# A two-block float32 network on one core: instruction order taken from the framework's time-line simulation, modulation tiles moved out of the SSD mixer

## The chip, the cores and the metric

The kernel runs on one core of one Trainium2 chip. The core has a matrix engine (TensorE, PE in the profile), a vector engine (VectorE, DVE), an activation engine (ScalarE, ACT), a general engine (GpSimd, POOL) and DMA queues, here issued by SyncE (SP). Each engine works through one list of instructions in the order in which the list was written; engines wait for each other by semaphores. The metric is the device time of one execution in microseconds. Before the change it is 1647.56 us, the median of three runs (1647.04 to 1647.98).

## The reference, cut to what matters

512 tokens of 1024 float32 channels pass two blocks.

```python
# block 1
mod = silu(c) @ w_ada + b_ada                 # 6 x 1024 numbers: shift, scale and gate, twice
h = rms_norm(x, norm1_w) * (1 + scale1) + shift1
q, k, v, xBC, z, dt_raw, gates = split(h @ w_in)
attn = block_attention(rope(norm(q)), rope(norm(k)), v)      # 16 heads, 4 k/v heads
ssd  = ssd_mixer(xBC, z, dt_raw, ...)         # conv + SiLU, 4 groups of 8 heads, both directions,
                                              # chunks of 128, times SiLU(z), rms_norm
merged = sigmoid(ga) * (attn @ w_attn_out) + sigmoid(gs) * (ssd @ w_ssd_out)
x = x + gate1 * (merged @ w_o)
x = x + gate2 * (square(relu((rms_norm(x) * (1 + scale2) + shift2) @ w_mlp1)) @ w_mlp2)
# block 2
x = x + rglru_layer(x)     # conv, gated linear recurrence
x = x + mla_layer(x)       # attention with compressed k/v, 8 heads
return rms_norm(x, final_norm)
```

## The kernel before, in words

All large products are float32 made of three products in a shorter format: `mm3` (L172) issues L174 (high by high), L175 and L176 (the two cross terms). A weight tile of 512 KB comes by DMA into the buffer pool `wr`, ACT casts its high part (L162, `wh`), and DVE or POOL subtracts the low part (L165, `wl`). The three pools have four buffers each. Every product of 512 columns accumulates in a PSUM tile `pm`, of which there are four; other results in PSUM are named `px`, `pf`, `pg`.

The modulation numbers `mod` are 48 columns of `modc`. Each is made by `mod_tiles` (L274): one DMA of a 512 KB tile of `w_ada` into a buffer of the pool `wr`, and one DVE instruction with an accumulated sum (L279). Columns 0 to 15 are needed for `h`, at the start. Columns 16 to 47 are needed only behind the merge, where `mod_cols` (L1380) and `gate_rows` (L934) read them. `MODS` (L43) says how many of them are made in each of the four SSD groups: 0, 0, 6 and 10. Attention makes the next eight and the merge one in each of its eight steps.

The SSD mixer runs over four groups. `ssd_core` (L553) goes through the steps of `CORE` (L41), and between them `ssd` (L676) issues the *fill*: products that nothing in this group waits for soon (`xbc` and `z` of the next group, `ssd_out` of the one before). The steps are states S, mixers M and outputs Y:

```python
# S: state of one chunk
nc.tensor.matmul(p, lhsT=Btm[:, c], rhs=xw, ...)                         # L598, xw by DVE L596
self.e("st").tensor_tensor(out=v8(st), in0=v8(prev[d]), in1=dcy, ...)    # L603 (DVE)
nc.vector.tensor_tensor(out=st, in0=st, in1=p, op=ALU.add)               # L604
nc.tensor.matmul(p, lhsT=CT[:, ...], rhs=st, ...)                        # L608
# M: mixer of one head: PE pf, pg (L623); per chunk ACT L629, DVE L631, ACT, DVE L635;
#    then ACT exp L642 and POOL e = e * w (L643)
# Y: output of two heads: PE L650, L653 (reads both e); then
nc.vector.scalar_tensor_tensor(out=yd, in0=xsT[j], ..., in1=y, ...)      # L657
nc.vector.scalar_tensor_tensor(out=yd, in0=yd, ..., in1=zt, ...)         # L659
nc.scalar.activation(out=hi, in_=yd, func=AF.Identity, scale=nw)         # L669, yh
nc.vector.scalar_tensor_tensor(out=lo, in0=yd, ..., in1=r32(hi), ...)    # L670, yl
```

`ssd_out` multiplies all four pairs (yh, yl) of a group by weights. In attention a head is four score products (L844, L845 into `px`), row maxima on DVE (L755), exponentials on ACT, scaling on POOL (L763), sixteen transposes (L851), the split into `ph` (ACT) and `pl` (DVE, L170), and the products with v (L859, L860). Its fill is q/k/v of the next k/v head and the gate products.

The order of instructions on each engine is not that of the source. When the `TileContext` of L1523 closes, the framework's scheduler orders them all, with the source's order as priority, and writes one list per engine.

Of the kernel before, what the change touches and what calls it, by code (L numbers as in the profile page):

```python
# [39 lines left out]
AORD = "s0 s1 s2 s3 f0 t0 m0 t1 m1 t2 m2 t3 m3 f1".split()  # L40
CORE = "S0 S1 M0 S2 S3 M1 S4 S5 M2 M3 Y0 M4 M5 Y1 M6 M7 Y2 Y3"  # L41
NC = 19
MODS = [0, 0, 6, 10]  # L43
WP = 0
TP = 0
LO = {"start": 5, "ssd": 8, "attn": 2, "merge": 3, "mlp": 0, "rglru": 3, "mla_in": 6, "mla": 5}
# [13 lines left out]
class Build:  # L60
# [616 lines left out]
    def ssd(self, first):  # L677
# [22 lines left out]
        for g in range(4):  # L700
# [5 lines left out]
            else:  # L706
# [3 lines left out]
                fill = so + zs + [lambda: next(q0, None)] * Q0  # L710
            k0 = 16 + sum(MODS[:g])
            k1 = k0 + MODS[g]
            fill = [lambda f=f, i=i: (f(), self.mod_tiles([k0 + i] if k0 + i < k1 else [])) for i, f in enumerate(fill)]
# [123 lines left out]
    def attention(self):  # L837
        nc = self.nc

        def scores(h, t):  # L840
            stk, (kh, kl), vv = self.qk[h // 4]
            p = self.ps()
            s = slice(t * 128, t * 128 + 128)
            nc.tensor.matmul(p, lhsT=stk[h % 4][:, s], rhs=kh, start=True, stop=False)  # L844
            nc.tensor.matmul(p, lhsT=stk[h % 4][:, s], rhs=kl, start=False, stop=True)  # L845
            return self.softmax_tile(p, 512)

        def turn(pr, kt):
            p = self.ps()
            for t in range(NT):  # L850
                nc.tensor.transpose(out=p[:, t * 128:t * 128 + 128], in_=pr[t][:, kt * 128:kt * 128 + 128],  # L851
                                    identity=self.ident)
            ph, pl = self.t("ph", F32R), self.t("pl", F32R)
            self.split(ph, pl, p)
            return ph, pl

        def mix(h, po, kt, parts):
            vv, (ph, pl) = self.qk[h // 4][2], parts
            nc.tensor.matmul(po, lhsT=vv[:, kt], rhs=ph, start=kt == 0, stop=False)  # L859
            nc.tensor.matmul(po, lhsT=vv[:, kt], rhs=pl, start=False, stop=kt == 3)  # L860

        def output(h, po):

            if h % 2 == 0:
                self.of = self.t("of")
            of = self.of
            d = slice(64 * (h % 2), 64 * (h % 2) + 64)
            e = slice(64 * (1 - h % 2), 64 * (1 - h % 2) + 64)
            nc.scalar.copy(out=of[d], in_=po[e])
            nc.vector.tensor_tensor(out=of[d], in0=of[d], in1=po[d], op=ALU.add)  # L870
            if h % 2 == 1:
                self.split(self.oh[:, h // 2], self.ol[:, h // 2], of)

        gates = [lambda m=m: self.gate_ssd(m) for m in range(8)]
        mods = list(range(16 + sum(MODS), 40))

        def fill(what):
            with self.fills():
                for x in what:
                    if x == "q":  # L880
                        next(nxt, None)
                    elif x == "g" and gates:
                        gates.pop(0)()
                    elif x == "m" and mods:
                        self.mod_tiles([mods.pop(0)])

        pr = [scores(0, t) for t in range(NT)]
        for h in range(16):
            g, i = divmod(h, 4)
            if i == 0:  # L890
                nxt = self.qkv(g + 1) if g < 3 else iter(())
            last = pr
            if i == 3:
                fill("q" * 8)
            pr = []
            po = self.pm() if POM else self.ps()
            turned = {}
            for x in AORD:
                j = int(x[1])
                if x[0] == "s" and h < 15:  # L900
                    pr.append(scores(h + 1, j))
                elif x[0] == "t":
                    turned[j] = turn(last, j)
                elif x[0] == "m":
                    mix(h, po, j, turned.pop(j))
                elif x[0] == "f":
                    fill(ATT[g][2 * i + j])
            output(h, po)
        fill("g" * 8 + "m" * len(mods))

    def merge(self):
        nc, a = self.nc, self.a
        oh, ol, acc, mh, ml = self.oh, self.ol, self.accS, self.mh, self.ml
        for m in range(8):
            gt = []
            self.gate_tile(m, gt)
            th = gt[0]

            def evac(i, ps):
                nc.vector.scalar_tensor_tensor(out=th, in0=th, scalar=1.0, in1=ps, op0=ALU.add, op1=ALU.mult)  # L920
                nc.vector.tensor_tensor(out=th, in0=th, in1=acc[:, m], op=ALU.add)
                self.split(mh[:, m], ml[:, m], th)

            self.gemm_cm([[a["w_attn_out"][m]]], lambda k: (oh[:, k], ol[:, k]), evac)
            self.mod_tiles([40 + m])

    def gate_rows(self, j, s):
        nc, a = self.nc, self.a
# [598 lines left out]
```

## Time and profile before

| | |
|---|---|
| median of three runs | 1647.56 us |
| the profiled execution | 1645.17 us |
| its span, first to last instruction | 1643.4 us |
| mean granted clock of TensorE | 0.995 |
| busy: PE / DVE / ACT / POOL | 96% / 69% / 48% / 27% |

The span is one execution seen by the profiler; 1.8 us lie around it. PE is busy nearly throughout, so the time is PE's work and the short pauses in it. The stages by time: modulation, norm and first products up to about 80 us, the SSD mixer to about 500, attention to about 720, the merge to about 840, then output projection, MLP and block 2.

### The profile page before, as it was taken

The page shows a single profiled execution, that of the slowest core. Times are in us where ns is not written, and L with a number is a line of the kernel's source. Part 1 is how long each engine was busy: PE and PEld are TensorE (multiplying, and loading weights), DVE is VectorE, ACT ScalarE, POOL GpSimd, SP SyncE. Part 2 cuts the span into 40 slices and gives each one's busy share as a digit, 9 for nine tenths or more (in the row PEclk, how much of TensorE's full clock was granted, in tenths as well). Part 3 has the DMA queues.
Part 4 walks back from the last instruction along what each step waited for, and adds up shares of the span by engine and source line. Part 5 has one row for each costly group of instructions (what it writes and reads, how often), then busy time and mean ns, then how long its engine had stood idle before and what let it go on. Part 6 is the DMA issues. An engine that isn't in the chain of part 4 may idle for free.

```text
span 1643.4 us, 20885 instructions
## 1 busy us (share of the span) xinstructions
PE 1579.3 (96%) x7696; PEld 1279.9 (78%) x7696; DVE 1126.8 (69%) x1948; ACT 789.5 (48%) x1517; POOL 446.5 (27%) x322
## 2 busy tenths in 40 slices
PE   5989999999999999999999999999999999999998
PEld 3767677677688778778889888888888778988886
DVE  6899689689869988874454344343458884747873
ACT  4347546355465667663344232322337662455652
POOL 3414345254252344321133011111141011321012
PEclk9999999999999999999999999999999999999999
DMA  7511124224222222215323232323323222322211
GB/s 255 197 57 60 52 87 130 66 82 146 78 77 91 71 71 90 78 52 192 103 64 116 90 103 91 102 90 103 112 70 99 87 90 67 100 69 71 64 62 52
DMA packets 50648, 153.54 MB, mean 93 GB/s; under 512 B 8177, under 2 KB 12913, under 8 KB 50546
## 3 DMA queue, kind: packets, MB, share of 16 engines
q1 hardware_dynamic: 50546, 152.22, 28.9%
q8 instruction: 60, 0.98, 0.2%
q14 instruction: 42, 0.34, 0.1%
HBM read 150.10 MB, written 2.10 MB: 93 GB/s over the span
## 4 chain that ended last, share of the span: by engine, by line
PE 72%; DVE 16%; ACT 4%; issue 3%; POOL 3%; DMA 1%; SPq 0%; DVEq 0%; POOLq 0%; ACTq 0%
PE pm L174 19%; PE pm L175 19%; PE pm L176 19%; DVE acc L507 2%; PE px L608 1%; DVE wada L279 1%; DVE nmax L755 1%; DVE wl L165 1%; PE px L851 1%; PE px L598 1%; POOL rs L254 1%; DVE w L635 1%; PE px L860 1%; PE px L653 1%; PE px L650 1%
## 5 line engine op out<-in xcount | busy, mean ns | idle before, releaser
L162 ACT CAST wh<-wr 128x1024 fp32r<-128x1024 f32 (+5 forms) x245 | 239.5, 980 | 390.3 <-PE pm L175 176.0
L165 DVE TENSOR_TENSOR wl<-wr,wh 128x1024 fp32r<-128x1024 f32 (+2 forms) x170 | 201.6, 1187 | 182.3 <-ACT wh L162 181.6
L165 POOL TENSOR_TENSOR wl<-wr,wh 128x1024 fp32r<-128x1024 f32 (+3 forms) x75 | 175.9, 2347 | 530.6 <-ACT wh L162 483.3
L174 PE MATMUL pm<-hh,wh 128*128 128x512 f32 (+1 forms) x432 | 172.9, 404 | 7.9 <-ACT hh L169 6.2
L175 PE MATMUL pm<-hl,wh 128*128 128x512 f32 (+1 forms) x432 | 175.0, 405 | 3.4 <-POOL hl L170 3.4
L176 PE MATMUL pm<-hh,wl 128*128 128x512 f32 (+1 forms) x432 | 172.4, 399 | 0.0
L986 POOL TENSOR_TENSOR r<-r 128x512 f32<-128x512 f32 x32 | 50.9, 1589 | 252.3 <-ACT r L985 252.3
L174 PE MATMUL pm<-h,wh 128*128 128x512 f32 (+1 forms) x288 | 105.4, 366 | 0.0
L175 PE MATMUL pm<-h,wh 128*128 128x512 f32 (+1 forms) x288 | 105.2, 365 | 0.0
L176 PE MATMUL pm<-h,wl 128*128 128x512 f32 (+1 forms) x288 | 105.2, 365 | 0.0
L174 PEld LDWEIGHTS pm<-hh,wh 128*128 128x128 f32 (+1 forms) x432 | 81.2, 188 | 29.4 <-ACT hh L169 7.6
L175 PEld LDWEIGHTS pm<-hl,wh 128*128 128x128 f32 (+1 forms) x432 | 81.6, 189 | 26.1 <-POOL hl L170 6.3
L174 PE MATMUL pm<-wh,rh 128*128 128x512 f32 x256 | 99.8, 390 | 0.0
L763 POOL TENSOR_SCALAR pr<-pr,psum 128x512 f32<-128x512 f32 x64 | 64.6, 1021 | 129.1 <-DVE psum L759 71.1
L176 PE MATMUL pm<-wh,rl 128*128 128x512 f32 x256 | 99.6, 389 | 0.0
L175 PE MATMUL pm<-wl,rh 128*128 128x512 f32 x256 | 99.6, 389 | 0.0
L176 PEld LDWEIGHTS pm<-hh,wl 128*128 128x128 f32 (+1 forms) x432 | 81.5, 189 | 19.7 <-issue 3.1
L507 DVE SCALAR_TENSOR_TENSOR acc<-pm,conv_w_s,acc 128x510 f32<-128x510 f32 (+2 forms) x114 | 84.5, 741 | 9.0 <-ACT acc L498 8.0
L643 POOL TENSOR_TENSOR e<-e,w 128x512 f32<-128x512 f32 x32 | 52.0, 1625 | 100.5 <-ACT e L642 74.5
L279 DVE SCALAR_TENSOR_TENSOR wada<-wada,cs 128x1024 f32<-128x1024 f32 x48 | 66.3, 1390 | 15.6 <-DMA wada<-in_w_ada 15.3
L758 ACT ACTIVATE pr<-px,nmax 128x512 f32<-128x512 f32 (+2 forms) x96 | 60.4, 637 | 29.9 <-DVE nmax L755 24.0
L174 PE MATMUL pm<-ha,wh 128*128 128x512 f32 (+1 forms) x192 | 68.2, 355 | 0.0
(401 smaller groups left out, 4130.1 us busy)
## 6 DMA issues: line engine op xcount, KB each, us to landing
wr<-in_w_mlp SPq DMA_DIRECT2D x64, 512.0 KB, 3.4
wada<-in_w_ada SPq DMA_DIRECT2D x48, 512.0 KB, 3.9
wr<-in_w_xbc SPq DMA_DIRECT2D x24, 512.0 KB, 3.5
wr<-in_w_in_a SPq DMA_DIRECT2D x20, 512.0 KB, 3.5
wr<-in_w_z SPq DMA_DIRECT2D x16, 512.0 KB, 3.5
wr<-in_w_ssd_out SPq DMA_DIRECT2D x16, 512.0 KB, 3.5
wr<-in_w_gate SPq DMA_DIRECT2D x16, 512.0 KB, 4.0
wr<-in_w_qkv SPq DMA_DIRECT2D x16, 384.0 KB, 3.1
```

Of the source, the lines that this page charges most:

```text
L162: nc.scalar.copy(out=hi[:, :n], in_=raw[:, :n])
L165: eng.tensor_tensor(out=lo[:, :n], in0=raw[:, :n], in1=r32(hi[:, :n]), op=ALU.subtract)
L174: m(out, lhsT=lh, rhs=rh, start=start, stop=False)
L175: m(out, lhsT=lh, rhs=rl, start=False, stop=False)
L176: m(out, lhsT=ll, rhs=rh, start=False, stop=stop)
L254: g.tensor_tensor(out=r, in0=r, in1=self.mhalf.to_broadcast(list(ss.shape)) if len(ss.shape) == 2 else self.mhalf.unsqueeze(2).to_broadcas ...
L279: nc.vector.scalar_tensor_tensor(out=w, in0=w, scalar=1.0, in1=self.cs, op0=ALU.mult, op1=ALU.mult, accum_out=self.modc[:, j:j + 1])
L507: nc.vector.scalar_tensor_tensor(out=acc[:, lo:hi], in0=ps[:, lo + o:hi + o], scalar=w[:, j:j + 1], in1=acc[:, lo:hi], op0=ALU.mult, op1=A ...
L643: self.e("ew").tensor_tensor(out=e, in0=e, in1=w, op=ALU.mult)
L758: nc.scalar.activation(out=e[:, :n], in_=p, func=AF.Exp, bias=nmax, accum_out=s)
L763: self.e("norm").tensor_scalar(out=e[:, :n], in0=e[:, :n], scalar1=s, scalar2=1.0, op0=ALU.mult, op1=ALU.mult)
L986: self.e("sq").tensor_tensor(out=r, in0=r, in1=r, op=ALU.mult)
```

## The change

`MODS` becomes all zeros, so that no modulation tile is made in the SSD groups; attention makes columns 16 to 23; each merge step makes three columns in place of one, 24 in all in place of eight. `TileContext` is given `schedule_with_timeline_sim=True`: the framework's scheduler then orders the instructions by its time-line simulation. What is computed is the same: the same count of instructions on each engine (PE 7420, DVE 1902, ACT 1375, POOL 327, SP 354), in another order.

```diff
-MODS = [0, 0, 6, 10]
+MODS = [0, 0, 0, 0]
...
-        mods = list(range(16 + sum(MODS), 40))
+        mods = list(range(16, 24))
...
             self.gemm_cm([[a["w_attn_out"][m]]], lambda k: (oh[:, k], ol[:, k]), evac)
-            self.mod_tiles([40 + m])
+            self.mod_tiles([24 + m, 32 + m, 40 + m])
...
-    with tile.TileContext(nc) as tc:
+    with tile.TileContext(nc, schedule_with_timeline_sim=True) as tc:
         emit(tc, a, out)
```

Three places show the order on PE. The numbers behind names tell buffers apart; where a number is the same before and after, it is the same tile, and `hh_102`, `hl_103` are the two parts of `h`.

The first place is the state steps of SSD group 0. Before, PE's list there (`pm_1138` is a fill product):

```order
L598 MATMUL px_907<-xw_905,Btm_720 128x512
L176 MATMUL pm_1059<-hh_102,wl_1062 128x512
L174 MATMUL pm_1138<-hh_102,wh_1140 128x512
L175 MATMUL pm_1138<-hl_103,wh_1140 128x512
L176 MATMUL pm_1138<-hh_102,wl_1141 128x512
L174 MATMUL pm_1138<-hh_102,wh_1140 128x512
L175 MATMUL pm_1138<-hl_103,wh_1140 128x512
L176 MATMUL pm_1138<-hh_102,wl_1141 128x512
L608 MATMUL px_912<-st_909,th_635 128x512
L623 MATMUL pf_951<-csb,sel 128x512
```

After, the states of the steps S3, S4 and S5 and the mixers beside them:

```order
L598 MATMUL px_907<-xw_905,Btm_720 128x512
L608 MATMUL px_912<-st_909,th_635 128x512
L623 MATMUL pf_951<-csb,sel 128x512
L623 MATMUL pg_952<-csb,sel 128x512
L598 MATMUL px_977<-xw_975,Btm_720 128x512
L608 MATMUL px_982<-st_979,th_635 128x512
L598 MATMUL px_1027<-xw_1025,Btm_720 128x512
L608 MATMUL px_1032<-st_1029,th_635 128x512
L623 MATMUL pf_1035<-csb,sel 128x512
L623 MATMUL pg_1036<-csb,sel 128x512
L623 MATMUL pf_1093<-csb,sel 128x512
L623 MATMUL pg_1094<-csb,sel 128x512
```

In the new list L598 and the L608 that needs its result stand side by side, and the fill that stood around them stands earlier; in groups 1 to 3 the new list has some 5 to 7 us of PE's work between the two.

The second place is behind output Y0 of the same group (`px_1117`). Before:

```order
L653 MATMUL px_1117<-e_955,xtm_695 64x128
L650 MATMUL px_1117<-ident,yoff_776 128x128
L653 MATMUL px_1117<-e_833,xtm_695 64x128
L653 MATMUL px_1117<-e_955,xtm_695 64x128
L623 MATMUL pf_1178<-csb,sel 128x512
L174 MATMUL pm_1307<-hh_102,wh_1309 128x512
L175 MATMUL pm_1307<-hl_103,wh_1309 128x512
L623 MATMUL pg_1179<-csb,sel 128x512
L176 MATMUL pm_1307<-hh_102,wl_1310 128x512
L174 MATMUL pm_1307<-hh_102,wh_1309 128x512
```

After:

```order
L653 MATMUL px_1117<-e_833,xtm_695 64x128
L653 MATMUL px_1117<-e_955,xtm_695 64x128
L650 MATMUL px_1117<-ident,yoff_776 128x128
L653 MATMUL px_1117<-e_833,xtm_695 64x128
L653 MATMUL px_1117<-e_955,xtm_695 64x128
L623 MATMUL pf_1178<-csb,sel 128x512
L623 MATMUL pg_1179<-csb,sel 128x512
L623 MATMUL pf_1202<-csb,sel 128x512
L623 MATMUL pg_1203<-csb,sel 128x512
L174 MATMUL pm_1495<-yh_1134,wh_1490 128x512
L174 MATMUL pm_1509<-yh_1134,wh_1490 128x512
L174 MATMUL pm_1548<-yh_1134,wh_1543 128x512
```

Before, 68 rows of fill, mixers and the next output follow the last L653 of Y0 until `yh_1134` is read. After, it is read by the fifth row: the four L623 alone stand between. `pm_1495`, `pm_1509`, `pm_1548` and `pm_1562` are four products of `ssd_out`, one row of each in turn.

The third place is a head in attention. Before, behind its score products (`px_5804` is the last):

```order
L175 MATMUL pm_5818<-wl_5827,hh_102 128x384
L176 MATMUL pm_5818<-wh_5826,hl_103 128x384
L844 MATMUL px_5804<-stk_5401,stk_5530 128x512
L845 MATMUL px_5804<-stk_5409,stk_5530 128x512
L174 MATMUL pm_5817<-wh_5832,hh_102 128x384
L175 MATMUL pm_5817<-wl_5833,hh_102 128x384
L176 MATMUL pm_5817<-wh_5832,hl_103 128x384
L174 MATMUL pm_5817<-wh_5832,hh_102 128x384
L175 MATMUL pm_5817<-wl_5833,hh_102 128x384
```

After, another head (`px_5999` is its last score):

```order
L844 MATMUL px_5989<-stk_5353,stk_5545 128x512
L845 MATMUL px_5989<-stk_5361,stk_5545 128x512
L844 MATMUL px_5999<-stk_5353,stk_5545 128x512
L845 MATMUL px_5999<-stk_5361,stk_5545 128x512
L851 MATMUL px_6044<-ident,pr_5731 128x128
L851 MATMUL px_6044<-ident,pr_5741 128x128
L851 MATMUL px_6044<-ident,pr_5751 128x128
L851 MATMUL px_6044<-ident,pr_5761 128x128
L859 MATMUL px_5968<-ph_6049,v_5286 128x512
```

Before, rows of a q/k/v product (`pm_5817`, `pm_5818`) stand between the scores of a head and its transposes. After, the transposes of this head follow its scores at once, and no `pm` row stands in the whole head; six heads in all stand so, in three pairs, and the fill is gathered ahead of each pair.

## Rows read from the trace of the kernel before

**Rows 1.** The page's first two lines: span, busy time and instructions of each engine.

```profile
span 1643.4 us, 20885 instructions
PE 1579.3 (96%) x7696; PEld 1279.9 (78%) x7696; DVE 1126.8 (69%) x1948; ACT 789.5 (48%) x1517; POOL 446.5 (27%) x322
```

**Rows 2.** The page's chain that ended last, shares by engine.

```profile
PE 72%; DVE 16%; ACT 4%; issue 3%; POOL 3%; DMA 1%; SPq 0%; DVEq 0%; POOLq 0%; ACTq 0%
```

**Rows 3.** PE's waits: tile, line, releaser; us in all, times, longest.

```profile
PE px L608 <- DVE st L604: 6.9, 5, 2.5
PE px L844 <- DVE of L870: 3.8, 3, 1.4
PE px L471 <- issue: 3.3, 1, 3.3
PE px L807 <- DVE st L170: 2.8, 4, 1.4
PE px L598 <- DVE xw L596: 2.6, 2, 1.4
PE px L860 <- DVE pl L170: 2.0, 4, 0.9
PE pm L175 <- DVE yl L670: 1.8, 1, 1.8
PE pm L174 <- DVE acc L507: 1.7, 1, 1.7
PE px L653 <- POOL e L643: 1.3, 1, 1.3
```

**Rows 4.** Windows: length, busy time (instructions) per engine, granted clock, DMA share, GB/s.

```profile
80.00:500.00 420.00, 401.26 (x1882) 301.08 (x1880) 352.18 (x625) 219.54 (x481) 164.07 (x82) 0.99 0.26 82
720.00:840.00 120.00, 119.97 (x560) 98.04 (x559) 58.98 (x81) 44.04 (x69) 18.20 (x14) 1.00 0.36 119
960.00:1000.00 40.00, 40.00 (x178) 33.13 (x177) 13.90 (x15) 15.68 (x22) 12.51 (x8) 1.00 0.31 95
```

**Rows 5.** The same view, three windows of 4 us behind two pauses of PE.

```profile
92.00:96.00 4.00, 1.61 (x7) 1.55 (x7) 2.95 (x4) 0.38 (x2) 1.02 (x1) 0.79 0.44 131
96.00:100.00 4.00, 4.00 (x22) 3.41 (x21) 3.66 (x9) 3.21 (x7) 0.00 (x0) 0.78 0.00 0
172.00:176.00 4.00, 4.00 (x18) 2.79 (x18) 1.91 (x3) 1.91 (x4) 0.00 (x0) 0.61 0.01 3
```

**Rows 6.** Timeline, first SSD output: start, duration, engine, line.

```profile
143.52 0.44 PE L653 MATMUL px<-e,xtm 128*64 128x128 f32 x4
...
144.50 0.74 DVE L657 SCALAR_TENSOR_TENSOR yd<-th,ssd_D_s,px 128x512 f32<-128x512 f32 x1
...
145.28 2.33 POOL L643 TENSOR_TENSOR e<-e,w 128x512 f32<-128x512 f32 x1 [1.89 <-DVE yd L657]
145.76 0.68 DVE L659 SCALAR_TENSOR_TENSOR yd<-yd,zt 128x512 f32<-128x512 f32 x1
...
146.96 1.73 DVE L165 TENSOR_TENSOR wl<-wr,wh 128x1024 fp32r<-128x1024 f32 x1
147.01 0.71 ACT L669 ACTIVATE yh<-yd,ssd_norm_w_s 128x512 fp32r<-128x512 f32 x1
148.61 0.74 DVE L670 SCALAR_TENSOR_TENSOR yl<-yd,ssd_norm_w_s,yh 128x512 fp32r<-128x512 f32 x1
```

**Rows 7.** DVE by line and form: count, busy us, mean ns, idle before.

```profile
L279 DVE SCALAR_TENSOR_TENSOR wada<-wada,cs 128x1024 f32<-128x1024 f32 x48 | 66.3, 1390 | 15.6 <-DMA wada<-in_w_ada 15.3 <-issue 0.2
L170 DVE TENSOR_TENSOR pl<-px,ph 128x512 fp32r<-128x512 f32 x72 | 48.2, 685 | 9.7 <-ACT ph L169 8.6
L755 DVE TENSOR_REDUCE nmax<-px 128x1 f32<-128x512 f32 x72 | 47.5, 680 | 9.4 <-PE px L845 8.9
L604 DVE TENSOR_TENSOR st<-st,px 128x512 f32<-128x512 f32 x16 | 10.9, 681 | 0.9 <-PE px L598 0.6
```

**Rows 8.** The page's groups: the POOL product that ends a mixer.

```profile
L643 POOL TENSOR_TENSOR e<-e,w 128x512 f32<-128x512 f32 x32 | 52.0, 1625 | 100.5 <-ACT e L642 74.5
```

## The prediction

> **What bounds the kernel now.** I read the page's first lines, then the chain, then PE's waits, then windows. PE is busy 1579.3 of 1643.4 us [rows 1], and PE has 72% of the chain, DVE 16% [rows 2]; so 64 us of pauses is all that an order can win, and every pause that it adds counts in full. Where PE has no pause, 178 matmuls fill 40.00 us [rows 4], 0.225 us for one of 512 columns; that is my price for a row of fill. The waits show where the pauses are [rows 3]: in the SSD mixer the state steps (L608 behind L604, 6.9 us; L598, 2.6), 3.3 us ahead of L471, and 4.8 at its outputs and mixers (L175 behind yl 1.8, L174 behind acc 1.7, L653 behind e 1.3); in attention 8.6 (L844 3.8, L807 2.8, L860 2.0). DVE is the second engine: in the SSD stretch it is busy 352 of 420 us, 84% [rows 4].
>
> The sum is made against the profiled execution, 1645.17 us; the median of the runs is 2.4 us above it, and I add that at the end.
>
> **State steps.** In the new list groups 1 to 3 have 5 to 7 us of PE's work between an L598 and its L608. L604 takes 0.68 us [rows 7] and no wait there was longer than 2.5 [rows 3], so those waits go: 6.9 + 2.6 = 9.5. In group 0, three pairs stand side by side with no work between. The least price of a pair is L604's 0.68, the most 2.5; I take 1.2 and 3.6 for the three, since DVE has other work there. Net -5.9, between -7.5 and -2.0.
>
> **L471.** The new list has 24 rows of fill ahead of it, 5.4 us of work, against a pause of 3.3; that goes. [...] Net -5.0; none of it if the fill ahead of it merely moves the pause.
>
> **Outputs.** This is the largest term. The fill that covered them stands earlier, ahead of the states and mixers. One output's chain as it ran [rows 6]: the last L653 ends at 143.96, yh is ready at 147.72, yl at 149.35, 5.4 us later. The first four rows that read yh (four `pm` tiles, 0.9 us) need no yl, so PE needs 4.5 us of other work between the last L653 and the first reader. Counted over the new list at 0.225 a row, it has, for the four outputs of each group: 0.9, 0.9, 2.9, 4.0 (group 0), 9.8, 1.6, 4.3, 4.0, then 12.8, 3.0, 4.3, 4.0, and 0.9, 0.9, 2.3, 3.0 (group 3). What lacks to 4.5 adds up to 9.3 + 3.6 + 2.2 + 10.9 = 26.0. The same count over the list before has 4.0, 4.0 and 4.1 as its least and gives 1.4, where 1.8 was measured [rows 3]: so the 4.5 is about right. What was late inside the chain was DVE's queue: an L165 of 1.73 us stood ahead of L670 [rows 6]. Lower bound: with nothing queued the chain is its four instructions, 0.74 + 0.68 + 0.71 + 0.74, and 0.54 of start, 3.4; PE then needs 2.5, and 7.7 us are lacking. Upper bound: another 1.1 us of DVE's queue, 5.6, and some 41 are lacking. I take 26.0, nearest to the measured chain. A second count agrees: from mixer 1 to the last yl of group 0, DVE has 36 us of work at its mean durations, PE 24; from mixer 2 in group 3, 36 against 22. DVE works in order, so PE cannot be done sooner. The 4.8 us of waits there before are part of this count and are taken off: net +21.2, between +2.9 and +36.
>
> [...] In the new list the outputs stand close to the mixers, so L659 and L670 (two inputs in SBUF) meet POOL's L643. One such meeting is shown: L643 began at 145.28 and took 2.33 us [rows 6] against a mean of 1.63 [rows 8], and L659, begun second, took 0.68 within it. So POOL was slowed by 0.7 us and DVE not held. [...]
>
> **Attention.** Six heads in three pairs stand without fill. In the third pair, from the first score of the one head to the last pl of the next product, DVE's new list has 8 L755 (0.68), 11 L170 (up to 0.685), 3 L279 (1.39) [rows 7] and 16 short ones: about 17 to 19 us, less 0.07 each where neighbours overlap; PE has 12 there. Excess 5 to 7 us; the other pairs give 4.1 and 4.5. I take 14, in place of the 8.6 of waits before: +5.4. Between -4 (DVE runs ahead during the bursts of fill) and +13 (the last heads, also nearly bare, wait as well).
>
> **The modulation tiles.** 16 tiles leave the SSD groups and join the merge: 16 x 1.39 = 22 us of DVE and 8.4 MB. From 720 to 840 us DVE is busy 59 of 120, the DMA engines 0.36 at 119 GB/s [rows 4], or 14.3 MB in 43 us of transfer; 8.4 MB more make 69 of 120. Both have room, and merge PE work hides them. But the tiles pass through the four buffers of `wr` that also bring the weights: +2, between 0 and +8. The freed DVE time in groups 2 and 3 is in the counts above; where it lets every queue drain, it is in the lower bounds.
>
> **Clock.** A pause of PE is followed by a fall: the two windows above, and 0.61 in the window behind L653's wait, 0.39 x 4 = 1.6 us [rows 5]. That second pause is one of those counted off. With the new pauses of 3 to 4 us I expect three more falls: 3 x 1.7 - 1.6 = +3.4, between -1.6 and +7.
>
> **Sum.** -5.9 - 5.0 + 21.2 + 5.4 + 2 + 3.4 = +21.1. 1645.2 + 21.1 + 2.4 = 1668.7, so 1669 us, 1.3% slower. All lower bounds: -15; all upper: +62 (L471 at 0). The stages behind the merge barely move; I price them at 0.
>
> **Rivals.**
> 1. *The waits go and the outputs are absorbed* (faster). DVE has 22 us less in groups 2 and 3, so its queue may be empty when an output comes. If the chain from L653 to yl is 3.4 us rather than 5.4 and the bare heads cost no more than the 8.6 before, the sum is the lower bounds: 1645 - 15 + 2.4, about 1632. It decides from some 10 us of lacking cover downwards. For it: the state waits surely go. Against: DVE's own count in groups 0 and 3.
> 2. *POOL and DVE hold each other* (much slower): if each of L659 and L670 waits for a whole L643 of 1.63, the six outputs with under 2 us of cover wait 6 x 2 x 1.63 = 20 us more: 1688. [...] Against it is the L659 that ran in 0.68 us [rows 6].
> 3. *The buffers of wr bind the merge*: if the three modulation tiles of a step hold the weights back by one L279 each (1.39 a step, 8 steps), 11 more: 1680. For it: four buffers, and a tile is freed only by DVE in its order. Against: DVE is half idle there.
> 4. *The pauses only move*: what the states and L471 give, 11 us, is what outputs and heads take, with the output term between its lower bound and mine: 1645 to 1650, no change (within 0.2%, about what a measurement of this kernel can tell).
>
> **How the numbers follow.** Forecast 0.50, rival 1 0.22, rival 2 0.10, rival 3 0.09, rival 4 0.09. The forecast's own range, outputs lacking 12 to 32 and the rest by up to 10 more, is 1655 to 1685. For 8 in 10 the range takes in rival 4, most of rivals 2 and 3, and the upper half of rival 1: 1637 to 1692. Faster by over 0.2% (below 1644.3): 0.22; within: 0.09; slower (above 1650.9): 0.69.
>
> **What would show it.** In the new profile: L608 behind L604 under 4 us and only in group 0; no pause at L471; L174 and L175 behind yh and yl as the largest group of PE's waits, 20 us or more, in groups 0 and 3; L844, L860 and L851 behind DVE and ACT in three places of attention; granted clock below 1 in more windows of the SSD stretch. I am wrong if PE's busy share stays at 96%, if the yh and yl waits stay under 8 us, or if the time is lost in the merge or behind it.

## The result, and the profile after

The changed kernel takes 1769.12 us (median of four runs; 1767.49 to 1771.28), against 1647.31 before (the three runs given above and one more): 1.074 times as long (95% interval 1.0721 to 1.0758). The prediction had the direction and about a sixth of the size: 1669 us, between 1637 and 1692.

The first lines of the page after answer to [rows 1]; span, then busy time and instructions of each engine:

```profile
span 1766.5 us, 20932 instructions
PE 1625.4 (92%) x7696; PEld 1319.0 (75%) x7696; DVE 1125.8 (64%) x1948; ACT 785.8 (44%) x1517; POOL 420.1 (24%) x322
```

The span is 123.1 us longer. It divides in two: PE's pauses grew from 64.1 to 141.1 us (+77.0), and PE's busy time grew by 46.1 us though it does the same 7696 matmuls. The second part is the clock: the mean granted clock fell from 0.995 to 0.959.

PE's waits after answer to [rows 3]; tile, line, releaser, then us in all, times, longest:

```profile
PE px L859 <- ACT ph L169: 13.6, 9, 2.7
PE pm L174 <- ACT yh L169: 11.7, 3, 9.1
PE pm L174 <- DVE acc L507: 11.7, 4, 5.1
PE pm L174 <- ACT yh L669: 10.3, 6, 2.4
PE px L807 <- DVE st L170: 7.5, 5, 1.8
PE pm L174 <- DVE sg L1039: 7.4, 2, 3.9
...
PE px L608 <- DVE st L604: 5.8, 3, 3.4
...
PE px L481 <- DVE cst L170: 5.6, 1, 5.6
...
PE px L561 <- DVE th L516: 4.1, 2, 3.9
PE px L860 <- DVE pl L170: 3.9, 2, 3.1
PE px L844 <- ACT pr L758: 3.5, 5, 1.0
...
PE px L471 <- PE pm L176: 0.4, 1, 0.4
```

No group is large; there are many. The outputs of the SSD mixer (`yh L669`) are 10 us of them. Attention has 28.5 in four groups (L859, L807, L860, L844; 8.6 before). Three groups have most of their time in the RG-LRU of block 2, where they are new: 9.3 of `acc`, `sg`, and 9.1 of `yh L169`.

By stage, length and PE's pauses in it, both worked out from the two traces. A stage ends where the first or last matmul or *evacuation* named in the table stands; an evacuation is the instruction of ACT or DVE that reads a finished product out of its PSUM tile, so that the tile can be used again.

| stage (its end) | before: us, paused | after: us, paused | longer by |
|---|---|---|---|
| start (80 us) | 80.0, 18.3 | 80.0, 17.0 | 0 |
| setup and SSD (first L844) | 438.2, 18.8 | 478.5, 37.1 | 40.3 |
| attention and merge (last L934) | 297.8, 10.0 | 334.7, 36.7 | 36.9 |
| output projection, MLP (first L1038) | 423.8, 2.2 | 431.4, 6.3 | 7.6 |
| RG-LRU (first L1217) | 245.5, 6.2 | 279.2, 26.8 | 33.7 |
| MLA (to 2.9 us before the end) | 155.2, 5.6 | 159.8, 14.2 | 4.6 |

The longest pauses are in the RG-LRU. The whole stage, before and after (length, then busy time of PE, PEld, DVE, ACT and POOL, granted clock, DMA share, GB/s), and its largest wait before:

```profile
1239.80:1485.30 245.50, 239.26 (x1133) 199.16 (x1132) 169.75 (x248) 133.90 (x214) 46.70 (x35) 1.00 0.27 86
```

```profile
1324.60:1603.80 279.20, 252.36 (x1155) 211.00 (x1154) 176.83 (x279) 135.71 (x219) 47.16 (x36) 0.95 0.24 76
```

```profile
PE px L174 <- ACT xh L169: 3.8, 3, 1.5
```

The timeline after, around one of the pauses (start, duration, engine, line, out<-in; in brackets the idle time of the engine just before, and what ended it):

```profile
1404.66 0.69 ACT L1081 ACTIVATE thr<-px,b_rg_s 128x512 f32<-128x512 f32 x1 [4.61 <-PE px L176]
...
1405.67 0.43 DVE L170 TENSOR_TENSOR wgl<-wg,wgh 128x256 fp32r<-128x256 f32 x1 [6.49 <-ACT wgh L169]
...
1406.83 0.77 ACT L498 ACTIVATE acc<-pm,conv_b_s,conv_w_s 128x512 f32<-128x512 f32 x1
1407.49 1.04 ACT L162 CAST wh<-wr 128x1024 fp32r<-128x1024 f32 x1
1407.63 1.53 DVE L507 SCALAR_TENSOR_TENSOR acc<-pm,conv_w_s,acc 128x509 f32<-128x509 f32 x2 [0.68 <-ACT acc L498]
...
1411.10 0.76 PE L174 MATMUL pm<-ha,wh 128*128 128x512 f32 x1 [5.10 <-DVE acc L507]
1411.66 0.63 PE L175 MATMUL pm<-ha,wh 128*128 128x512 f32 x1
1412.09 0.63 PE L176 MATMUL pm<-ha,wl 128*128 128x512 f32 x1
```

Three engines wait for one another here. ACT waited 4.61 us for a gate product of PE (L1081); L498, which evacuates another product, stands behind that gate in ACT's list. DVE waited 6.49 us for ACT. Then PE waited 5.10 us, because its next product needs the tile that L498 and L507 empty. Behind the pause, matmuls start 0.43 us apart in place of 0.225: from 1408.6 to 1415.4 the granted clock was 0.50.

The clock, window by window (columns as above), around that pause:

```profile
1404.00:1408.00 4.00, 2.00 (x9) 1.31 (x7) 1.49 (x3) 3.34 (x6) 0.00 (x0) 1.00 0.40 138
1408.00:1412.00 4.00, 0.90 (x2) 0.83 (x3) 3.93 (x6) 2.18 (x4) 0.00 (x0) 0.57 0.14 15
1412.00:1416.00 4.00, 4.00 (x12) 3.07 (x11) 2.39 (x5) 2.45 (x2) 0.00 (x0) 0.57 0.29 116
1416.00:1420.00 4.00, 4.00 (x19) 3.14 (x17) 4.00 (x5) 0.00 (x0) 0.00 (x0) 1.00 0.00 0
```

Such falls answer to [rows 5]; each is a stretch of 3.41 or 6.83 us at a granted clock of 0.50. Behind the first 80 us, and up to the last 3, the trace after has 23 of them (17 of 6.83 us), the trace before 2 (both of 3.41). Summed over the whole span, the time at 0.50 times 0.5 is 73 us after and 8 before. Part of it lies in the pauses themselves, where it costs nothing; over PE's busy time alone it is 56 and 6, enough for the 46 by which the busy time grew.

### The profile page after: what moved, and what is told of

The parts are those of the page before. It is cut to its first block, busy times and chain, and to the rows that moved or that the text cites. A ratio compares the mean times of both kernels' runs of the same rounds, so it can differ in the third digit from the quotient of the medians.

```text
span 1766.5 us, 20932 instructions
## 1 busy us (share of the span) xinstructions
PE 1625.4 (92%) x7696; PEld 1319.0 (75%) x7696; DVE 1125.8 (64%) x1948; ACT 785.8 (44%) x1517; POOL 420.1 (24%) x322
## 3 DMA queue, kind: packets, MB, share of 16 engines
q1 hardware_dynamic: 50546, 152.22, 26.7%
## 4 chain that ended last, share of the span: by engine, by line
PE 74%; DVE 13%; ACT 5%; DMA 3%; issue 2%; POOL 1%; SPq 0%; DVEq 0%; POOLq 0%; ACTq 0%
PE pm L174 21%; PE pm L175 20%; PE pm L176 20%; DMA wada<-in_w_ada 2%; DVE acc L507 2%; DVE wl L165 1%; PE px L608 1%; DVE wada L279 1%; PE px L598 1%; PE px L650 1%; PE px L653 1%; PE px L175 1%; PE px L174 1%; ACT pr L758 1%; PE px L176 1%
## 5 line engine op out<-in xcount | busy, mean ns | idle before, releaser
L162 ACT CAST wh<-wr 128x1024 fp32r<-128x1024 f32 (+5 forms) x245 | 239.3, 982 | 398.0 <-PE pm L175 159.0
L165 DVE TENSOR_TENSOR wl<-wr,wh 128x1024 fp32r<-128x1024 f32 (+2 forms) x170 | 203.4, 1197 | 202.2 <-ACT wh L162 195.9
L165 POOL TENSOR_TENSOR wl<-wr,wh 128x1024 fp32r<-128x1024 f32 (+3 forms) x75 | 167.9, 2242 | 649.7 <-ACT wh L162 583.3
L174 PEld LDWEIGHTS pm<-hh,wh 128*128 128x128 f32 (+1 forms) x432 | 81.6, 190 | 26.8 <-ACT hh L169 6.6
L507 DVE SCALAR_TENSOR_TENSOR acc<-pm,conv_w_s,acc 128x510 f32<-128x510 f32 (+2 forms) x114 | 84.6, 744 | 24.2 <-ACT acc L498 22.9
L176 PEld LDWEIGHTS pm<-hh,wl 128*128 128x128 f32 (+1 forms) x432 | 81.4, 188 | 20.1 <-issue 2.9
L763 POOL TENSOR_SCALAR pr<-pr,psum 128x512 f32<-128x512 f32 x64 | 59.4, 941 | 148.2 <-DVE psum L759 144.1
L755 DVE TENSOR_REDUCE nmax<-px 128x1 f32<-128x512 f32 (+2 forms) x96 | 58.6, 618 | 33.9 <-PE px L845 32.8
```

The costliest lines, as they stand in the source:

```text
L162: nc.scalar.copy(out=hi[:, :n], in_=raw[:, :n])
L165: eng.tensor_tensor(out=lo[:, :n], in0=raw[:, :n], in1=r32(hi[:, :n]), op=ALU.subtract)
L174: m(out, lhsT=lh, rhs=rh, start=start, stop=False)
L176: m(out, lhsT=ll, rhs=rh, start=False, stop=stop)
L507: nc.vector.scalar_tensor_tensor(out=acc[:, lo:hi], in0=ps[:, lo + o:hi + o], scalar=w[:, j:j + 1], in1=acc[:, lo:hi], op0=ALU.mult, op1=A ...
L755: nc.vector.tensor_reduce(out=nmax, in_=p, axis=AX.X, op=ALU.max, negate=True)
```

## The experiments

Theory at the start: the new order alone makes the loss. It takes away *cover*, the work that PE has between a result's last input and its first reader; so PE pauses, and each pause is paid twice, once as itself and once through the clock. Rivals: the modulation tiles, and one engine's list at fault.

**The two halves of the change.** Ordering alone, tiles where they were:

```diff
-    with tile.TileContext(nc) as tc:
+    with tile.TileContext(nc, schedule_with_timeline_sim=True) as tc:
```

> The kernel before with schedule_with_timeline_sim=True alone; the modulation tiles stay where they were. Theory A (the new order takes the fill early, leaves PE bare in many places, and each pause also lowers the granted clock; the tiles hardly matter): 1745 to 1775 us, 0 to 25 us from the changed kernel's 1769. Theory B (the moved tiles, with three per merge step through the four weight buffers, cost a good part): 1690 to 1730 us.

Measured 1770.36, ratio 1.0755 (1.0734 to 1.0775): the order alone makes as large a loss. Tiles moved, old ordering:

> The modulation tiles moved as in the change, the order by the old scheduler. Theory A: 1640 to 1655 us, within 0.5% of before. Theory B: 1670 us or more, with PE's waits in the merge behind weights (L174 to L176 behind wh or wl).

Measured 1644.63, ratio 0.999 (0.998 to 0.9999), and once more:

> The kernel before with the modulation tiles moved as in the change, and its old ordering, once more with more rounds: 1644 to 1646 us, ratio 0.998 to 0.9995, if the 0.1% of the first run was a gain; 1647 to 1648 if it was chance.

1644.72, ratio 0.9989 (0.998 to 0.9997). In the old order the tiles cost nothing; they save some 2 us.

By stage the two halves do depend on each other. With the new order and the tiles unmoved, setup and SSD take 492.4 us (47.3 of pauses), attention and merge 320.5 (28.8). With the tiles moved as well these are 478.5 (37.1) and 334.7 (36.7), with the same count of matmuls in each. So in the new order the move takes 13.9 us from the one stage and adds 14.2 to the other, one profiled execution each, and the sum hides it.

**Is the count of the outputs' cover right?** In the kernel before, `NC = 19` becomes `NC = 12`, so that less fill is left for the outputs.

> The kernel before, old scheduler, with one number changed: NC = 12 instead of 19, so that the fill of each SSD group is issued within its first 12 steps. On PE the work between an output's last L653 and the first reader of its yh becomes nearly that of the changed kernel (0.9, 1.1, 3.7, 3.6; 6.3, 1.6, 3.7, 3.6; 6.3, 1.6, 3.5, 3.3; 0.9, 1.4, 4.2, 3.6 us), while the state steps stay as before. Theory A (where the fill stands is the cause, pauses bring the clock down): by the prediction's 4.5 us an output, 26 us are lacking and each of some 7 pauses costs 1.7 to 3.4 of clock on top: 1675 to 1695 us. Rival (the loss in SSD is from what the time-line order does on the other engines): 1645 to 1655 us.

Measured 1689.65, ratio 1.0271 (1.0254 to 1.0288). PE's waits and busy time:

```profile
PE 1597.8 (95%) x7696; PEld 1288.3 (76%) x7696; DVE 1128.1 (67%) x1948; ACT 790.3 (47%) x1517; POOL 439.3 (26%) x322
PE pm L174 <- ACT yh L669: 20.2, 7, 7.2
...
PE pm L175 <- DVE yl L670: 2.8, 4, 1.4
```

The rule of 4.5 us of cover lets 24.9 us more be lacking here than before; PE's pauses grew by 24.4. The sum agrees, and the waits for yh stand, as counted, nearly all at the six outputs with the least cover. Single ones don't agree: they run from 1.3 to 7.2 us where 2.9 to 3.6 was lacking, so that the sum comes out so close is in part luck. PE's busy time grew by 18.5 on top, with a granted clock of 0.981 against 0.995: the clock adds 0.76 us per us of pause. Setup and SSD grew by 38.8 us, near the 40.3 of the changed kernel, so the place of the fill alone can make a loss of this size there.

**What does a pause cost?** In the kernel before, nine products of the dense MLP get weights of which DVE first rewrites one column, with a value from the product before; nothing else is changed. In the one form the value comes from that product's PSUM tile, and the pause is short; in the other it comes from `r` behind POOL's square, and the pause is longer:

```diff
+    def after(self, wh):
+        self.hold is not None and self.nc.vector.scalar_tensor_tensor(out=wh[:, 0, 0:1], in0=self.hold[:, 0:1], scalar=0.0, ...
...
-                    wh, wl = self.weight(ap, gain)
+                    wh, wl = self.weight(ap, gain); self.after(wh)
...
-                nc.scalar.activation(out=r, in_=ps, func=AF.Relu)
+                nc.scalar.activation(out=r, in_=ps, func=AF.Relu); self.hold = ps if ch and m in (1, 3, 5) else None
```

(the longer one has `r` in place of `ps`)

> The kernel before with nine added waits in the dense MLP: in three of its four chunks, three products of the first MLP matrix have one DVE instruction on one column of their high weight part (it adds zero times the first column of the product before, read from PSUM), so PE stops from the end of that product until DVE is through, some 0.5 to 1 us. Theory A (a pause of 1.5 us or more lowers the granted clock, a shorter one does not): PE idle +5 to +9 us, PE busy +0 to +2, time +5 to +11. Rival 1 (any pause lowers the clock): busy +15 or more. Rival 2 (the clock costs nothing of its own): as theory A here.

> The same nine waits, but the column is that of r after its square on POOL (1.6 us), so each pause is 2.5 to 3.5 us. Theory A: PE idle +22 to +32 us, and each of nine pauses brings a stretch of 3.4 us at the lower clock, 1.7 lost: PE busy +12 to +18, time +35 to +48. Rival 1 (any pause lowers the clock): as here, but the short ones too. Rival 2 (the clock costs nothing of its own): idle as here, busy +0 to +3.

Measured 1673.08 (1.0158; 1.0142 to 1.0173) and 1698.6 (1.0312; 1.0289 to 1.0335). Of the short one, PE's busy time, the wait, and two windows at a pause; then the same of the long one:

```profile
PE 1583.5 (95%) x7696; PEld 1279.5 (77%) x7696; DVE 1128.1 (68%) x1957; ACT 789.3 (47%) x1517; POOL 445.3 (27%) x322
PE pm L174 <- DVE wh L147: 20.4, 9, 2.3
...
1072.00:1076.00 4.00, 1.72 (x8) 1.09 (x8) 1.38 (x3) 1.54 (x2) 1.40 (x1) 1.00 0.13 54
1076.00:1080.00 4.00, 4.00 (x19) 3.33 (x18) 0.69 (x1) 0.62 (x1) 0.18 (x1) 1.00 0.38 131
```

```profile
PE 1598.8 (94%) x7696; PEld 1291.2 (76%) x7696; DVE 1128.9 (67%) x1957; ACT 789.8 (47%) x1517; POOL 445.6 (26%) x322
PE pm L174 <- DVE wh L147: 30.4, 9, 3.4
...
1080.00:1084.00 4.00, 0.61 (x3) 0.27 (x2) 1.38 (x2) 2.09 (x3) 1.58 (x1) 0.81 0.07 20
1084.00:1088.00 4.00, 4.00 (x10) 3.17 (x11) 0.69 (x1) 0.07 (x1) 0.00 (x0) 0.50 0.30 111
1088.00:1092.00 4.00, 4.00 (x16) 3.25 (x16) 0.00 (x0) 0.10 (x1) 0.00 (x0) 0.84 0.00 0
```

Nine pauses of 2.3 us cost the pauses and little more: +25.8 of span, of it 20.4 waits and 4.2 busy time; two of the nine were followed by a fall. Nine of 3.4 us: +50.7, of it 30.4 waits and 19.5 busy time, with a fall behind seven. So 1.1 us more per pause brought 1.7 us more busy time each (15.3 / 9). That a pause is paid twice is shown, for the longer ones. Both medians are above what was expected, the short one because its pauses came out longer than I had reckoned. The 1.5 us of theory A did not hold: seven of nine pauses of 2.3 us had no fall behind them.

**Is it the pauses or the low load at the outputs?** The kernel after, with a matmul on `yd` behind each of the 16 outputs (its sum is not used), to keep PE at work there:

```diff
-                                           op1=ALU.mult)
+                                           op1=ALU.mult); nc.tensor.matmul(y, lhsT=self.ident, rhs=yd, start=True, stop=True, skip_group_check=True)
```

> The changed kernel with one more float32 matmul per SSD output, 16 in all (some 0.86 us each, 14 us of PE work): it multiplies yd by the identity into the output's own px tile, which nobody reads any more, so it can only run between L659 and the products with yh. Theory A (the fall of the clock behind a pause is a cost of its own): the added work lies in the pauses and keeps the clock up, 1750 to 1766 us, and fewer than half of the stretches with a granted clock below 1 between 150 and 530 us. Rival (the pauses alone cost, the clock follows them and costs nothing of its own): 1769 to 1783 us.

Measured 1785.77 (1.0845; 1.0822 to 1.0868). The new matmuls waited themselves, 9.5 us in seven places, and the falls stayed (72 us summed as above, against 73). Both forecasts missed: a filler that reads the late tile is one more waiter.

**Is it the place of the fill on PE?** In the kernel before, the fill of attention gathered in the first four of eight slots of a head (`e_att_burst`); and the RG-LRU's products issued two steps ahead (`e_rg_ahead2`):

```diff
-ATT = ["qm q q q qm q qg g".split(), ...
+ATT = ["qmqq qqqm qg g - - - -".split(), ...
```

> The kernel before, old scheduler, with attention's fill issued in the first four of the eight slots of each k/v head (ATT), so that two to three heads of each group have little fill. Theory A: waits behind ph, pl, pr and st grow by 10 us or more and the clock falls in some places: 1655 to 1675 us. Rival (attention's heads are covered by each other's transposes; its loss in the changed kernel is from the modulation tiles and DVE's order): 1643 to 1652 us.

```diff
-            if i >= 2:
-                product([(xin, i)])
+            if 2 <= i + 2 <= 9:
+                product([(xin, i + 2)])
... (the product of gin likewise)
```

> The kernel before, old scheduler, where the RG-LRU loop issues the products xin and gin of step i+2 in step i, so that the gates of the last two steps stand without fill on PE, as in the changed kernel. Theory A: PE waits behind acc, sg and yh at the end of the layer and the clock falls there: 1662 to 1680 us. Rival (the +22 us in RG-LRU of the changed kernel come from another thing, table loads or the DVE order): 1645 to 1655 us.

Measured 1655.03 (1.0057; 1.0042 to 1.0072) and 1651.42 (1.0038; 1.0023 to 1.0053). Bursts of fill give 10 of the 37 us that attention and merge lost, all of it in that stage (297.8 to 307.9); the early products give 4 of 34. Neither, made in this way, is the main cause.

**Can the products be paced?** In the kernel after, the weights of the RG-LRU's products, and in another those of the SSD's fill, are loaded only when the gates of one or two steps before, or the work six steps before, are done (POOL writes one column of the buffer from that tile ahead of the load):

```diff
+    def wait_for(self, raw):
+        self.pace is not None and self.nc.gpsimd.tensor_copy(out=raw[:, 0:1], in_=self.pace[:, 0:1])
...
-        nc.sync.dma_start(out=v[0], in_=ap)
+        self.wait_for(raw); nc.sync.dma_start(out=v[0], in_=ap)
```

> The changed kernel, where in the RG-LRU layer the weights of a product of step i (xin, gin) are loaded only when the gates of step i-2 or i-1 are through (a one-column copy by POOL into the weight buffer ahead of its DMA). That puts the fill of the last steps back behind the gates. Theory A: PE's waits between 1360 and 1485 us behind acc, sg and yh (28 us) shrink to under 8 and the clock there stays at 1: 1735 to 1752 us. Rival (the chain through DVE and ACT with its table loads sets the pace, whatever stands between): 1764 to 1774 us.

> The changed kernel, where the weights of SSD fill are loaded only when the step of six marks ago is through (a one-column copy by POOL into the weight buffer). The new order then has 5.7 us or more behind every output, but no work between L598 and L608 in ten of 24 states. Theory A: the output waits (yh, yl, e) go, with their clock, and ten state pairs cost 1 to 2.5 each: 1745 to 1765 us. Rival (weights become late and PE waits for them, as pacing did in the RG-LRU layer): 1775 us or more, with L174 behind wh as the largest wait.

Measured 1793.54 (1.0889; 1.0863 to 1.0914) and 1773.19 (1.0774; 1.0755 to 1.0793). In the first the waits for `acc` and `sg` went, but PE then waited for weights:

```profile
PE pm L174 <- ACT wh L162: 35.2, 11, 6.4
```

In the second too the largest wait is for weights (15.2 us, the same line). The theory missed both times, as the weights came too late, so the question stayed open.

**Is it PE's list, or do the lists have to agree?** In the kernel after, PE's list in the RG-LRU, or in the SSD mixer, held in the order in which the program issues it; in the SSD mixer each state step is also cut in two, as the expectation says:

```diff
-            with ExitStack() as R:
+            with ExitStack() as R, tc.manual_schedule(engines={mybir.EngineType.PE}):
```

> The changed kernel with PE's list alone kept in the order of the source within the RG-LRU layer; all else by the time-line simulation. Theory A1 (PE's list runs ahead there until its four product tiles are full and wait for ACT and DVE): freed tiles follow the end of a product within 10 us instead of 13 to 32, the waits behind acc, sg and yh shrink to under 10 us: 1742 to 1756 us. Rival A2 (the lists of ACT and DVE, which put an evacuation behind instructions that wait for PE, are the cause): they stay so, 1762 to 1785 us.

> The changed kernel with PE's list kept in the order of the source within the SSD mixer, the source changed there so that the second half of a state step (L603 to L615) is issued one step later, with the fill between. The outputs then have 4.2 us of PE's work or more behind them, 16 of 24 states 5.4 us and 8 none. All else by the time-line simulation. Theory A (PE's list there is the cause): SSD takes 400 to 412 us from the first L623 to the first score instead of 426, in all 1740 to 1762 us. Rival (the other engines' lists): 1765 us or more.

Measured 1810.04 (1.0985; 1.0967 to 1.1003) and 1841.84 (1.1189; 1.117 to 1.1207). Both worse. In the first a gate stands right behind the product that it needs, and PE waits there:

```profile
PE px L174 <- ACT xh L169: 45.4, 9, 7.4
```

In the second it waits 29.4 us ahead of L598 and 18.3 ahead of L471, so this order too has losses of its own.

So the same with products two steps ahead, for PE alone, and for all five engines:

> The kernel after, with PE's list in the RG-LRU held in an order written out by hand: each pair of products two steps ahead of the gates that use them, as in the list before. The lists of the other engines are still made by the simulation. Theory (what counts is that the lists of PE, ACT and DVE agree in which product an engine turns to next): the simulation lines ACT and DVE up with PE's fixed list, but by its own durations; part of the stage's 34 us comes back, 1745 to 1765 us. Rival (ACT's and DVE's lists alone do the harm): no gain, 1765 to 1790. The earlier hand order with no lead, in which each gate stood right behind its product, gave 1810.

> The same, with the lists of all five engines in the RG-LRU held in that one written order. Theory: no engine stands before an instruction that waits for a later one of another engine's list, the products' PSUM tiles are freed within some 8 us of the product's end as before, the RG-LRU takes 245 to 258 us with under 12 us idle in place of 279 with 26.8, and the whole 1735 to 1750. Rival (the loss in the RG-LRU comes from the stages ahead of it or from what the simulation does on both sides of it): the stage stays over 268 us, the whole at or above 1760.

Measured 1793.81 (1.0899; 1.088 to 1.0918) and 1954.99 (1.1878; 1.1862 to 1.1895). Of the first, then of the second:

```profile
PE px L174 <- ACT xh L169: 21.3, 9, 4.3
...
PE px L175 <- DVE xl L170: 13.1, 9, 2.8
```

```profile
PE pm L174 <- ACT wh L162: 61.4, 19, 13.2
PE px L174 <- ACT xh L169: 58.9, 10, 9.5
```

The theory missed twice. In the second PE waits for the splitting of weights (L162), which in the program's own order is not done ahead of its product; it has a loss of its own and does not tell whether lists that agree would do.

**Late evacuations alone.** I counted over the lists, at 0.225 a row, how much more of PE's list an evacuation of the RG-LRU has to wait for than its own product, because of what stands ahead of it on its engine: summed, ACT 2 and DVE 5 us before, ACT 141 and DVE 107 after. The kernel before, with products two steps ahead and evacuations held back behind the gates; with two held back the sums are 109 and 106, with one 24 and 5:

```diff
-                         lambda m, ps: jobs[m][0](jobs[m][1], ps), halves=halves, mid=mid)
+                         lambda m, ps: held.append((*jobs[m], ps)) if mid is None else jobs[m][0](jobs[m][1], ps), halves=halves, mid=mid)
...
+            while len(held) > (2 if i < 7 else 0): f, j, p = held.pop(0); f(j, p)
```

> The kernel before, with its old ordering, products of the RG-LRU issued two steps ahead (that alone gave 1651), and the evacuation of a product by ACT and DVE issued late, behind the gates of the step, with two evacuations always held back. In ACT's list, summed over the 18 products of the steps, the evacuations then stand behind instructions that need 109 us more of PE's list than their own product (141 in the kernel after, 2 in the kernel before); in DVE's, 106 (107, and 5). Theory (late evacuations keep PE's product tiles full, and that is the loss in the RG-LRU): the stage grows by 20 to 40 us, idle by 12 to 25, PE waits for a tile that ACT frees, 1668 to 1695. Rival (place of evacuations is harmless, the loss is of another kind): 1649 to 1660.

> The same with one evacuation held back: in ACT's list the sum is 24 us, in DVE's 5, near the kernel before. Theory: little is lost, 1650 to 1660; that the written form itself costs something would show here as well. Rival: as with two held back, within 4 us of it.

Measured 1652.5 (1.0047; 1.0031 to 1.0064) and 1640.56 (0.9968; 0.9958 to 0.9979). PE's waits of the first in the RG-LRU:

```profile
PE pm L174 <- DVE acc L507: 6.5, 2, 4.5
PE pm L174 <- ACT yh L169: 2.7, 1, 2.7
```

Waits of two groups of the kernel after appear, the same lines and releasers, and between the two forms the stage differs by 12.4 us (252.7 and 240.3), with 8.6 more of pauses. But the expected 20 to 40 did not come, and the time lies in the rival's range: late evacuations make this kind of wait, and here they cost 12 us, where the stage lost 33.7 in the changed kernel. What makes the rest isn't shown.

The second is below both of its forecasts, and the fastest kernel of the study, 0.3% under the kernel before. Its RG-LRU takes 240.3 us in place of 245.5: PE's wait for `xh` (3.8 us, three times) is gone.

**State steps cut in two.** The kernel with the tiles moved and the old ordering, with a `yield` behind L598 so that the next item is issued before L608:

> The same, and each state step of the SSD mixer cut in two, so that the next item of the list is issued between its first product and the product that reads it. The list before has waits of 6.9 us at L608 and 2.6 at L598; if the cut takes most of them and nothing else moves: 1637 to 1642. If the pauses only move to the outputs, whose cover the cut takes: 1645 to 1652.

Measured 1647.34, ratio 1.0007 (0.9998 to 1.0016). L608's waits shrank from 6.9 us to 0.7 and L598's grew from 2.6 to 10.6:

```profile
PE px L598 <- DVE xw L596: 10.6, 8, 2.6
```

The pauses only moved.

## Why the prediction was wrong

Its sum was +21.1 us; the span grew by 123.1. By its own steps, with PE's pauses as measured (-2.8, +5.7, +15.3, +26.7, +33.3 and, at the start, -1.3 make the 77.0):

**State steps**, -5.9 predicted. L608 and L598 went from 9.5 to 6.7 us: -2.8. As foretold only group 0 waits at L608, in three places, but up to 3.4 us where I took 1.2.

**L471**, -3.3 of wait and -1.7 of clock. The 1.7, in the clock term also the price of a fall, is what the first two windows of [rows 5] lack of a clock of 1, (0.21 + 0.22) x 4 us; the trace before has it as 3.41 us at 0.50, from 94.35. The wait went to 0.4, but L481 now pauses 5.6 us and L561 4.1 (1.1 before): +5.7 in all, with a granted clock of 0.50 to 0.74 in four of the five windows between 96 and 116 us. The condition that I named, that the pause merely moves, held.

**Outputs**, +21.2. All waits of outputs and mixers in the SSD stretch went from 4.8 to 20.1 us: +15.3, within the bounds. The reads of `yh` and `yl` alone are 11.4, not the 20 or more that I asked for. The count gave the right sum in the old order with `NC = 12`, and too much in the new one, where six of the sixteen chains from the last L653 to yl took 4.2 to 4.6 us, worked out from the trace, against the 5.4 priced. Its check against the list before (1.4 counted, 1.8 measured) was luck: the measured wait stood at an output that had 6.3 us of PE's work behind it but whose yl came 9.7 us after the last L653, and none of the outputs counted as lacking had a pause of note.

**Attention and the modulation tiles**, +7.4. Pauses there grew by 26.7, twice the upper bound of attention's term. I had counted DVE's list; the largest group, 13.6 us, waits for ACT's `ph`. The moved tiles cost nothing there in the old order, but in the new one 14.2 of the stage's 36.9 us come with them, and I had looked for their price in the merge alone. The order by itself makes 22.7, and bursts of fill, made alone, 10. That the rest comes from the order of the other engines' lists, which I did not read there, is likely and not shown.

**Clock**, +3.4. This is a step that failed by its size: 46.1 us of busy time, and 23 falls behind the first 80 us where there had been two, in place of three more. I priced a fall at 1.7 us and allowed one for each of three pauses, where 17 of the 23 last 6.83 us, those before 3.41, and show 3.4, and each of the 17 pauses of 2 us and more behind the first 80 us has one, long or short. That a pause is followed by a fall did not hold throughout in the trace before: behind one of 2.49 us, from 219.64, the granted clock was 1.00. The pause that was to be counted was every pause in the program, not the three longest of one stage.

**The stages behind the merge**, priced at 0. This is the step that failed outright: 45.9 us longer, 33.3 of them pauses. I had read the new lists at the three places that the profile before made prominent, and took a stage without pauses as one that stays so. But the flag reorders every list. In the RG-LRU, which had 6.2 us of pauses, PE, ACT and DVE now wait for each other, with 26.8 us of pauses. The prediction's last sign of being wrong, time lost behind the merge, came true.

Three sums in the prediction are slightly off, by its own numbers, and change nothing: the lower bound's lack adds up to 7.5 us, not 7.7, the clock term to 3.5, and the second rival counts six outputs with under 2 us of cover where the list of covers has five, which makes 16 us in place of 20.

Of the rivals, the buffers of `wr` did not bind the merge: PE's pauses there are 0.0 us with the tiles moved in the old order, and 2.0 in the changed kernel. That DVE and POOL hold each other I had set aside on one meeting in which L659, begun second, was not slowed. The timeline after shows others:

```profile
309.47 1.59 POOL L643 TENSOR_TENSOR e<-e,w 128x512 f32<-128x512 f32 x1 [2.25 <-DVE w L635]
309.84 1.76 DVE L659 SCALAR_TENSOR_TENSOR yd<-yd,zt 128x512 f32<-128x512 f32 x1
...
312.47 1.27 POOL L666 TENSOR_TENSOR ssacc<-ssacc,sq 128x512 f32<-128x512 f32 x1 [1.42 <-ACT sq L665]
312.97 1.32 DVE L670 SCALAR_TENSOR_TENSOR yl<-yd,ssd_norm_w_s,yh 128x512 fp32r<-128x512 f32 x1 [1.37 <-ACT yh L669]
```

L643 ends at 311.06 and L659 0.54 us later; L666 ends at 313.74 and L670 0.55 later. Where no POOL instruction ran beside them they took 0.68 and 0.74 us, so these two lasted 1.08 and 0.58 us longer. Before, 11 of the 16 L659 began while a POOL instruction (L643 or L165) ran, and 10 of them ended 0.55 us after it; the eleventh, at 145.76, is the meeting that I relied on. As the reason for the loss the rival still falls: L670 met L666 in this way at 12 of the 16 outputs before as well as after, and L659's median went from 838 to 684 ns:

```profile
L659 DVE SCALAR_TENSOR_TENSOR yd<-yd,zt x16: 674/838/2147, 145.8 to 496.0; 128x512 f32<-128x512 f32 x16
```

```profile
L659 DVE SCALAR_TENSOR_TENSOR yd<-yd,zt x16: 675/684/1764, 176.5 to 532.6; 128x512 f32<-128x512 f32 x16
```

(before, then after; duration min, median, max in ns)

What is shown: the order alone makes the loss; lost cover at the SSD outputs makes a loss of the stage's size; longer pauses are paid again through the clock; late evacuations make waits of the kind seen in the RG-LRU. What stays open: which entries of ACT's and DVE's lists cost the rest in the RG-LRU (some 20 us) and in attention (some 13 of the 22.7 from the order alone), and how the moved tiles add 14.2 there in the new order only. Every attempt to put one list back made a loss of its own.

## What to carry to other kernels

A scheduler's switch changes every list in the program: read the new lists in the quiet stages too, and on each engine whose reader frees PE's tiles, before pricing any stage at nothing. Where PE is busy nearly all the time, add to each new pause what the clock takes behind it (here 0.6 to 0.8 us per us of pause, but 0.2 for the short ones in dense work), by counting all pauses. Cover that is only moved from one wait to another may win nothing: with the state steps cut in two the waits moved from L608 to L598, and the time stayed.

## What the runs showed of the hardware

Pauses of the same length are not followed by the same clock. In the dense MLP seven of nine pauses of 2.3 us had no fall behind them. In the SSD mixer after the change, a pause of 2.39 us ahead of 300.35, with small matmuls and a pause of 0.43 just before it, was followed by a window at 0.50:

```profile
296.00:300.00 4.00, 1.53 (x6) 0.69 (x5) 3.86 (x7) 2.69 (x5) 1.47 (x2) 0.91 0.39 131
300.00:304.00 4.00, 3.65 (x8) 2.65 (x9) 4.00 (x9) 4.00 (x16) 1.10 (x1) 0.50 0.02 4
304.00:308.00 4.00, 4.00 (x26) 2.63 (x24) 3.63 (x12) 2.04 (x6) 1.45 (x1) 0.74 0.00 0
```

What else than the length of the pause decides, the runs don't settle.
